# Repricing the matrix engine in a planned instruction order, and turning 64 x 64 blocks by products alone

## Chip, cores and metric

The kernel runs on one core of a Trainium2 chip. The metric is the device time of one execution in microseconds (us). The kernel before took a median of 3212.47 us in three runs (3202.04 to 3217.61).

## What is computed

One inference step of a two-layer decoder trunk, all in fp32, for 256 prompt positions and 8 sample rows that share the weights. They are laid side by side, so every activation has T = 264 columns.

```python
for i in range(DEPTH):
    h = rmsnorm(x, norm_mix[i])
    if i % 2 == 0:
        proj = h @ w_in_a[j]
        o_rwkv, sh, S = rwkv7_mix(proj[..., :RWKV_PROJ], ...)
        o_s5, hr, hi = s5_mix(proj[..., RWKV_PROJ:], ...)
        mix = jnp.concatenate([o_rwkv, o_s5], -1) @ w_out_a[j]
    else:
        mix, S = retention_mix(h @ w_in_c[j], st_ret[j], pos, ret_gn[j], w_out_c[j])
    x = x + mix
    x = x + swiglu(rmsnorm(x, norm_ffn[i]), w_gate[i], w_up[i], w_down[i])
```

Layer 0 mixes with RWKV-7 (16 heads of 64, worked as 8 pairs, in chunks of 64 positions) beside S5 (64 groups of states). Layer 1 mixes with retention.

## The kernel before, in words

**The stream.** All large matrix products are one list of tasks (`run_stream`, L555). A task is one 128-column tile of a weight. Four row blocks of 128 (a grain) arrive by one DMA; ScalarE rounds them to a high part `wh` (L478) and VectorE takes the low part `wl` (L479), and each block is multiplied in three passes, `wh*xh + wh*xl + wl*xh` (L578 to L580). So the stream is matmuls of a 128 x 128 weight with 264 columns, three for each block of 128 rows.

**The side work.** The mixers run beside the stream as Python generators ("sides"): S5, its output, the RWKV fronts, two interleaved RWKV backs, their ends, the sample rows (`rwkv_sample_half`, L1296), and in layer 1 `ret_mix` and `ret_sample`. Their calls are recorded as operations with dependencies (`issue`, L289).

**The order.** Nothing is scheduled on the chip: each engine runs its instructions in the order in which the planner emits them. The planner keeps a clock for each engine (`clk`, keys P, V, S, G and D for TensorE, VectorE, ScalarE, GpSimd and DMA), prices an instruction in `cost` (L213), finds when its operands are ready in `after` (L240), and advances the clock in `emit` (L258). After every second block of 128 rows, `pump` (L519) emits side operations that are ready by the planner's TensorE clock, up to a budget: 1.65 us of that clock in layer 0, 1.3 us in layer 1 (`MOST` times `PART` over `UK`). A stream task that needs a flag of a side has side operations forced out until the flag is there (`need`, L550).

**Prices of TensorE before** (L216 to L227): a stream matmul 0.113 us, a transposition 0.11 us or 0.04 us for 64 columns, a plain fp32 product of a 64-column weight with 64 columns 0.08 us. The price is doubled where the planner takes the clock for low (L273). A change of the tile size within the array has no price, and products on different quarters of the array are priced one after the other. VectorE, ScalarE, GpSimd and DMA have prices of their own (L228 to L238, L265), which the change leaves alone; a DMA is given 1.7 us and 0.03 us plus 1.11e-5 us an element.

**Blocks turned.** RWKV needs 64 x 64 blocks transposed. `turned` (L401) does a block that lands on partitions 0 to 63 by a transposition and one that lands on partitions 64 to 127 by a product with the identity. It is called in `front` (L885: 8 blocks a pair) and through `heads` in `back` for the first level (L946: 8 blocks, L951: 6 blocks, L956: 8 blocks). In all of these calls the two kinds alternate.

**The sample rows.** For each of the 8 pairs, `rwkv_sample_half` multiplies by a matrix of ones (L1349), lets VectorE and GpSimd work on the result (L1350, L1351), spreads a row over 64 partitions by two DMAs into the same tile (L1354), multiplies that tile on VectorE (L1356), adds on GpSimd (L1357), and goes back to TensorE (L1361).

Of the kernel before, what the change touches and what calls it, by code (L numbers as in the profile page):

```python
# [10 lines left out]
F32R = mybir.dt.float32r  # L11
# [9 lines left out]
T = TP + TS  # L21
# [20 lines left out]
FAR = 1 << 20  # L42
# [17 lines left out]
class Task:  # L60
    def __init__(self, w, row0, nk, c0, rhs, done, need=None):
        self.w, self.row0, self.nk, self.c0 = w, row0, nk, c0
        self.rhs, self.done, self.need, self.pre = rhs, done, need, None
# [64 lines left out]
class Builder:  # L128
    def __init__(self, ctx, tc, ins, outs, dumps=None):
        self.ctx, self.tc, self.nc = ctx, tc, tc.nc  # L130
        self.I, self.O, self.C0 = ins, outs, ins["cst"]
        self.dumps = dumps or {}
        self.side, self.rec = [], None
        self.evac = Side(None, -1)
        self.clk = dict.fromkeys("PVSGD", 0.0)
        self.where, self.uses, self.pend = {}, {}, {}
        self.tick, self.cols, self.warm = 0, 0.0, False
        self.flags = Flags(self)
        self.act_set = None
        nc = self.nc  # L140
        self.V, self.G, self.S, self.P = (Eng(self, e, k) for e, k in
                                          ((nc.vector, "V"), (nc.gpsimd, "G"), (nc.scalar, "S"), (nc.tensor, "P")))
        self.Q, self.QG, self.QS = (Eng(self, e, "D") for e in (nc.sync, nc.gpsimd, nc.scalar))
        pool = lambda name, **k: ctx.enter_context(tc.tile_pool(name=name, **k))
        self.pw = pool("pw", bufs=1)
        self.pc = pool("pc", bufs=1)
        self.pb = pool("pb", bufs=1)
        self.ps = pool("ps", bufs=1, space=PSUM)
        ctx.enter_context(tc.manual_schedule())
        self.banks = [self.ps.tile([128, 512], F32, name=f"ps{i}", tag=f"ps{i}") for i in range(8)]  # L150
        self.layer, self.held = 0, {}
        self.turn, self.bank, self.open, self.busy = 0, {}, [], [None] * 4
        for b in self.banks:
            self.cells(b)
# [58 lines left out]
    def cost(self, key, name, a):  # L213

        n = int(np.prod(a[0].shape[1:])) if hasattr(a[0], "shape") else 1
        if key == "P":  # L216
            w = a[2] if name == "transpose" else a[1]
            w = int(np.prod(w.shape[1:]))
            if a[1].dtype == F32R:
                return 0.113 * n / T  # L220
            if name == "transpose":
                return 0.11 if w > 64 else 0.04
            if w <= 32:
                return max(0.034, 0.02 + 0.42e-3 * n)
            if w <= 64:
                return max(0.08, 1.05e-3 * n)
            return max(0.205, 1.68e-3 * n)  # L227
        if key == "V":  # L228
            fast = name in ("tensor_scalar", "tensor_copy", "memset") and not any(str(x.space) == str(PSUM) for x in a if hasattr(x, "space"))
            c = 0.07 + n * (0.52e-3 if fast else 1.04e-3) + (0.006 * n if name == "reciprocal" else 0)  # L230
            if name.startswith(("tensor_scalar", "scalar")) and any(hasattr(x, "shape") and tuple(x.shape[1:]) == (1,) for x in a[2:]):
                c += 0.07
            return c
        if key == "S":
            return 0.094 + n * 0.83e-3
        if key == "D":
            return 0.03 + n * a[0].shape[0] * 1.11e-5
        return 0.035 + n * 0.83e-3 if name == "memset" else 0.15 + n * 2.05e-3  # L238

    def after(self, key, uses):  # L240

        t = 0.0
        for name, (at, bits), w in uses:
            if isinstance(name, int):
                b = self.bank[name].at
                if b is None:
                    name = min((self.banks[i].tensor.name for i in range(4) if not self.busy[i]), key=lambda n: self.uses[n].max())
                else:
                    name = self.banks[b].tensor.name
            u = self.uses[name]  # L250
            for q in (0, 1) if w else (0,):
                for e, k in enumerate("PVSG"):
                    v = u[q, e][at].max()
                    if v:
                        t = max(t, v + (LAG["P" in (k, key)] if k != key else 0.0 if key == "P" or q else 0.125))
        return t

    def emit(self, eng, name, a, k):  # L258

        a = [self.real(x) for x in a]  # L260
        key, uses = eng.key, self.operands(name, a, k)
        c = self.cost(key, name, a)
        t = self.after(key, uses)
        if key == "D":
            t = self.clk["D"] = max(t + 1.7, self.clk["D"]) + c  # L265
        else:
            if key == "P":
                while self.clk["P"] + 0.1 >= (self.tick + 1) * 3.4133:
                    self.warm = self.cols >= 3277
                    self.tick, self.cols = self.tick + 1, 0.0  # L270
                n = int(np.prod(a[0].shape[1:]))
                self.cols += n * (1 if a[1].dtype == F32R else 2 if name == "transpose" else 4) * a[1].shape[0] / 128
                c *= 1 if self.warm else 2  # L273
            elif key == "S":
                self.functions(ACT_SET.get(a[2]))
            t = self.clk[key] = max(self.clk[key], t) + c
        for n, (at, bits), w in uses:
            self.uses[n][0 if w else 1, "PVSG".index(key) if key != "D" else 3][at] = t
        getattr(eng.eng, name)(*a, **k)  # L279
        return t  # L280
# [119 lines left out]

    def turned(self, out, a, one):  # L401

        if out.offset % FAR < out.ap[0][0]:
            self.P.transpose(out, a, one)
        else:
            self.P.matmul(out, a, one, start=True, stop=True)

    def gcopy(self, out, a):
        self.G.tensor_scalar(out, a, 1.0, None, op0=OP.mult)
# [1399 lines left out]
```

## Time and profile before

| what | us |
|---|---|
| median of three runs | 3212.47 |
| lowest, highest run | 3202.04, 3217.61 |
| profiled execution | 3204.68 |
| its span | 3202.9 |
| TensorE busy in the span | 3121.3 |
| VectorE, ScalarE, GpSimd busy | 1972.0, 1498.7, 343.4 |

Every instruction of the planned order has the line of `emit` that issues it (L279), so groups are told apart by tile names and shapes. A form such as `64*64 64x64` is rows * columns of the weight, then partitions x columns of what streams past it. In `ps<-cst,ar_tmp` the operand that streams comes first: a block turned streams the constant identity, `cst`. A plain fp32 product leaves two records, a transposition or a stream matmul one. The timeline gives each piece's start and its duration with the pipeline's drain, so the cost of a piece is read from its start to the start of the next.

### The profile page before, as it was taken

What the parts mean: (1) busy time and instruction counts of PE and PEld (TensorE: products, weight loads), DVE (VectorE), ACT (ScalarE), POOL (GpSimd) and SP (SyncE); (2) the same over time, 40 slices, a digit from 0 to 9 for tenths busy, and PEclk for the clock granted to TensorE, in tenths of its full rate; (3) what the DMA queues carried; (4) which work ended last, traced back from release to release, by engine and by line L of the source; (5) the groups of instructions that cost most, each with busy time, mean ns of one, the idle gap of its engine ahead of it and who ended that gap; (6) DMA issues with size and microseconds to landing.
All of it is one profiled execution on the core that took longest, in us unless ns stands there. A gap on an engine that the chain in (4) does not pass through costs nothing.

```text
span 3202.9 us, 65844 instructions
## 1 busy us (share of the span) xinstructions
PE 3121.3 (97%) x26390; PEld 2967.3 (93%) x26390; DVE 1972.0 (62%) x3702; ACT 1498.7 (47%) x2733; POOL 343.4 (11%) x525
## 2 busy tenths in 40 slices
PE   7999798899999999999999999999999999999998
PEld 7987687799999999999998998988899999999998
DVE  6788666466555555566566666565566565555554
ACT  6543355255444444455344444444455444444454
POOL 5111332100000000001111111011100000000001
PEclk9999899799999999999999999999999999999999
DMA  5323413455655556666666677567666555565654
GB/s 192 120 86 74 61 54 70 84 163 183 179 184 180 182 179 184 181 182 211 216 230 219 230 250 254 174 244 250 217 179 184 181 182 184 178 183 180 184 179 152
DMA packets 161138, 560.54 MB, mean 175 GB/s; under 512 B 21312, under 2 KB 23744, under 8 KB 160576
## 3 DMA queue, kind: packets, MB, share of 16 engines
q1 hardware_dynamic: 140384, 483.29, 50.7%
q0 software_dynamic: 19584, 71.31, 5.9%
q8 instruction: 207, 3.39, 0.4%
q10 hardware_dynamic: 864, 1.74, 0.1%
q14 instruction: 99, 0.81, 0.1%
HBM read 511.45 MB, written 42.69 MB: 173 GB/s over the span
## 4 chain that ended last, share of the span: by engine, by line
PE 92%; DVE 3%; DMA 2%; ACT 1%; POOL 1%; issue 0%; SPq 0%; DVEq 0%; POOLq 0%; ACTq 0%
PE ps L279 92%; DMA ar_tmp<-ar_tmp 2%; DVE ar_tmp L279 1%; POOL ar_tmp L279 1%; DVE wl L279 1%; DVE t L279 1%; ACT ar_tmp L279 0%; ACT wh L279 0%; DVE ar_hidb L279 0%; DVE ar_hidy L279 0%; SPq L279 0%; DVE xl L279 0%; DVE ar_hida L279 0%; POOL ar_hida L279 0%; ACT L285 0%
## 5 line engine op out<-in xcount | busy, mean ns | idle before, releaser
L279 DVE TENSOR_TENSOR wl<-raw,wh 128x512 fp32r<-128x512 f32 x1784 | 1260.6, 710 | 904.1 <-ACT wh L279 892.5
L279 ACT ACTIVATE wh<-raw 128x512 fp32r<-128x512 f32 x1784 | 1098.9, 628 | 936.3 <-PE ps L279 905.5
L279 PE MATMUL ps<-xh,wh 128*128 128x264 f32 x4512 | 1330.0, 295 | 14.7 <-ACT wh L279 12.4
L279 PE MATMUL ps<-xh,wl 128*128 128x264 f32 x4512 | 1289.7, 286 | 10.8 <-DVE wl L279 10.7
L279 PE MATMUL ps<-xl,wh 128*128 128x264 f32 x4512 | 1287.8, 285 | 0.0
L279 PEld LDWEIGHTS ps<-xh,wh 128*128 128x128 f32 x4512 | 858.8, 190 | 63.4 <-issue 28.6
L279 PEld LDWEIGHTS ps<-xh,wl 128*128 128x128 f32 x4512 | 856.4, 190 | 12.6 <-DVE wl L279 12.6
L279 PEld LDWEIGHTS ps<-xl,wh 128*128 128x128 f32 x4512 | 860.0, 191 | 5.7 <-issue 4.8
L279 PE MATMUL ps<-hl,wh 128*128 128x264 f32 x1280 | 364.0, 284 | 0.0
L279 PE MATMUL ps<-hh,wl 128*128 128x264 f32 x1280 | 363.9, 284 | 0.0
L279 PE MATMUL ps<-hh,wh 128*128 128x264 f32 x1280 | 363.8, 284 | 0.0
L279 PE MATMUL ps<-n,wh 128*128 128x264 f32 x1408 | 257.4, 284 | 0.0
L279 PE MATMUL ps<-ar_tmp 64*64 64x64 f32 (+8 forms) x2912 | 215.3, 283 | 39.5 <-DVE ar_tmp L279 24.6
L279 PEld LDWEIGHTS ps<-hh,wh 128*128 128x128 f32 x1280 | 241.4, 189 | 0.0
L279 PEld LDWEIGHTS ps<-hl,wh 128*128 128x128 f32 x1280 | 240.9, 188 | 0.0
L279 PEld LDWEIGHTS ps<-hh,wl 128*128 128x128 f32 x1280 | 240.7, 188 | 0.0
L279 PEld LDWEIGHTS ps<-ar_tmp 64*64 64x64 f32 (+3 forms) x2912 | 149.3, 149 | 82.3 <-DVE ar_tmp L279 28.9
L279 POOL TENSOR_TENSOR sqs<-sq,sqs 128x264 f32<-128x264 f32 x56 | 42.4, 758 | 1663.5 <-ACT sq L279 1663.5
L279 PEld LDWEIGHTS ps<-n,wh 128*128 128x128 f32 x1408 | 217.8, 188 | 0.0
L279 PE MATMUL ps<-n,wl 128*128 128x264 f32 x704 | 199.6, 284 | 0.0
L279 PE MATMUL ps<-omh,wh 128*128 128x264 f32 x512 | 147.1, 287 | 0.0
L279 PE MATMUL ps<-omh,wl 128*128 128x264 f32 x512 | 145.6, 284 | 0.0
(214 smaller groups left out, 2872.1 us busy)
## 6 DMA issues: line engine op xcount, KB each, us to landing
raw<-in_w_in_c_dram SPq DMA_DIRECT2D x192, 512.0 KB, 4.3
raw<-in_ffn_w_gate_dram SPq DMA_DIRECT2D x176, 512.0 KB, 3.6
raw<-in_ffn_w_up_dram SPq DMA_DIRECT2D x176, 512.0 KB, 3.7
raw<-in_ffn_w_down_dram SPq DMA_DIRECT2D x176, 512.0 KB, 3.7
out_dram<-ar_tmp POOLq DMA_DIRECT2D x72, 512.0 KB, 4.3
raw<-in_w_in_a_dram SPq DMA_DIRECT2D x68, 512.0 KB, 3.7
ar_tmp<-in_state_ret_dram POOLq DMA_DIRECT2D x64, 512.0 KB, 6.9
raw<-in_w_out_c_dram SPq DMA_DIRECT2D x64, 512.0 KB, 3.8
```

The source lines that it names most:

```text
L279: getattr(eng.eng, name)(*a, **k)
```

## The change

Three things: new TensorE prices in `cost`; a tile size and a place in the array for each matmul (`tile_of`), by which `emit` adds a price for a change of size, and lets matmuls of one small size on different places overlap in the plan; and `turned` without its transposition. No constant of the planner changes (budgets, look-ahead, priorities), nor any price of another engine.

```diff
@@ def cost(self, key, name, a):
             w = int(np.prod(w.shape[1:]))
+            load = 0.004 + 0.833e-3 * w
             if a[1].dtype == F32R:
-                return 0.113 * n / T
+                return max(load, 0.005 + 0.44e-3 * n)
             if name == "transpose":
-                return 0.11 if w > 64 else 0.04
-            if w <= 32:
-                return max(0.034, 0.02 + 0.42e-3 * n)
-            if w <= 64:
-                return max(0.08, 1.05e-3 * n)
-            return max(0.205, 1.68e-3 * n)
+                return max(load, 0.42e-3 * n)
+            return 2 * max(load, 0.002 + 0.833e-3 * n)
...
+    def tile_of(self, name, a):
+
+        r = lambda n: 32 if n <= 32 else 64 if n <= 64 else 128
+        w = a[1]
+        m = 128 if name == "transpose" or w.dtype == F32R else r(int(np.prod(w.shape[1:])))
+        size = r(int(w.shape[0])), m
+        return size, (w.offset // w.ap[0][0], a[0].offset % FAR // a[0].ap[0][0])
...
@@ def emit(self, eng, name, a, k):
                 c *= 1 if self.warm else 2
+                size, at = self.tile_of(name, a)
+                t0 = max(self.clk["P"], t)
+                if size != self.size:
+                    t0 = max([t0, *self.tiles.values()]) + 0.09 + 0.833e-3 * size[1]
+                    self.size, self.tiles = size, {}
+                t0 = max(t0, self.tiles.get(at, 0.0))
+                t = self.tiles[at] = t0 + c
+                self.clk["P"] = t if size == (128, 128) else t0 + 0.012
             elif key == "S":
                 self.functions(ACT_SET.get(a[2]))
-            t = self.clk[key] = max(self.clk[key], t) + c
+            if key != "P":
+                t = self.clk[key] = max(self.clk[key], t) + c
...
     def turned(self, out, a, one):
 
-        if out.offset % FAR < out.ap[0][0]:
-            self.P.transpose(out, a, one)
-        else:
-            self.P.matmul(out, a, one, start=True, stop=True)
+        self.P.matmul(out, a, one, start=True, stop=True)
```

## Rows read from the trace of the kernel before

**Rows 1.** The page: span, TensorE's busy time, the chain by engine

```profile
span 3202.9 us, 65844 instructions
...
PE 3121.3 (97%) x26390; PEld 2967.3 (93%) x26390; DVE 1972.0 (62%) x3702; ACT 1498.7 (47%) x2733; POOL 343.4 (11%) x525
...
PE 92%; DVE 3%; DMA 2%; ACT 1%; POOL 1%; issue 0%; SPq 0%; DVEq 0%; POOLq 0%; ACTq 0%
```

**Rows 2.** Windows: length, busy us of PE, PEld, DVE, ACT, POOL; PEclk, DMA, GB/s

```profile
0.00:180.00 180.00, 154.45 (x1176) 148.21 (x1177) 135.06 (x303) 107.44 (x212) 55.54 (x101) 0.95 0.47 152
180.00:300.00 120.00, 117.56 (x1340) 100.32 (x1338) 104.25 (x310) 47.45 (x96) 21.09 (x36) 0.97 0.29 77
300.00:420.00 120.00, 98.83 (x1007) 81.95 (x1007) 76.20 (x192) 38.15 (x108) 40.05 (x65) 0.83 0.40 62
420.00:540.00 120.00, 117.56 (x1451) 97.50 (x1449) 81.79 (x214) 73.01 (x153) 41.81 (x68) 0.99 0.21 56
540.00:660.00 120.00, 102.43 (x1125) 85.82 (x1126) 59.39 (x132) 29.25 (x63) 17.01 (x18) 0.80 0.47 88
660.00:740.00 80.00, 79.83 (x659) 79.56 (x658) 59.11 (x106) 46.36 (x94) 10.65 (x15) 1.00 0.58 178
740.00:3202.00 2462.00, 2450.61 (x19641) 2373.95 (x19639) 1456.20 (x2448) 1157.06 (x2010) 157.29 (x224) 1.00 0.63 197
```

**Rows 3.** Groups by form: the matmuls of turned 64 x 64 blocks

```profile
L279 PE MATMUL ps<-cst,ar_tmp 64*64 64x64 f32 x192 | 30.6, 256 | 0.1
...
L279 PE MATMUL ps<-cst,ar_hida 64*64 64x64 f32 x75 | 11.3, 243 | 0.0
...
L279 PE MATMUL ps<-cst,ar_hidb 64*64 64x64 f32 x45 | 7.4, 260 | 1.3 <-DVE ar_tmp L279 1.3
...
L279 PE MATMUL ps<-cst,t 64*64 64x64 f32 x48 | 7.1, 243 | 0.0
```

**Rows 4.** PE timeline: two turned groups, of eight and of six blocks

```profile
184.11 1.36 PE L279 MATMUL ps<-cst,ar_hida 64*64 64x64 f32 x9
185.40 0.39 PE L279 MATMUL ps<-xh,wh 128*128 128x264 f32 x1
...
191.66 0.28 PE L279 MATMUL ps<-xh,wl 128*128 128x264 f32 x1
191.87 1.79 PE L279 MATMUL ps<-cst,ar_hida 64*64 64x64 f32 x12
193.59 0.70 PE L279 MATMUL ps<-ar_hidy,cst 128*128 128x256 f32 x2
```

**Rows 5.** PE timeline: groups of products alone, of eight and six blocks

```profile
242.20 0.68 PE L279 MATMUL ps<-ar_tmp 64*64 64x64 f32 x16 [0.67 <-DVE ar_tmp L279]
242.81 0.39 PE L279 MATMUL ps<-xh,wh 128*128 128x264 f32 x1
243.04 0.28 PE L279 MATMUL ps<-xl,wh 128*128 128x264 f32 x1
...
451.94 0.57 PE L279 MATMUL ps<-ar_hidb,ar_tmp 64*64 64x64 f32 x12 [0.33 <-DVE ar_tmp L279]
452.44 0.39 PE L279 MATMUL ps<-xh,wh 128*128 128x264 f32 x1
```

**Rows 6.** Waits of PE: waited for, us in total, times, longest

```profile
PE ps L279 <- DVE ar_tmp L279: 28.6, 13, 7.3
...
PE ps L279 <- POOL ar_tmp L279: 7.9, 1, 7.9
```

**Rows 7.** Pieces of the chain: the first and last row spread by DMA

```profile
293.02 10.07 DMA ar_tmp<-ar_tmp
...
578.78 10.08 DMA ar_tmp<-ar_tmp
```

**Rows 8.** PE timeline: first and last departure from the stream before 660 us

```profile
29.76 1.25 PE L279 MATMUL ps<-sqs,cst 128*128 128x264 f32 x2
...
658.60 0.60 PE L279 MATMUL ps<-ar_hidx,ar_hida 128*128 128x264 f32 x2
```

More of the change, by code (lines that the diff above doesn't have):

```diff
@@ L137, in __init__ @@
         self.tick, self.cols, self.warm = 0, 0.0, False
+        self.size, self.tiles = None, {}
         self.flags = Flags(self)
```

## The prediction, made before the changed kernel was run

> **What bounds the kernel now.** I read the page first: TensorE is busy for 3121 of 3203 us, and the chain that ends last runs over it for 92% [rows 1]. Then the windows, since such a share mixes stages with different limits [rows 2]. From 740 us on (both feed-forward blocks and layer 1) TensorE has 2451 busy us in 2462, one record every 0.125 us: there only fewer or cheaper matmuls help, and the change touches no block of that stretch except through the order. Up to 660 us, in layer 0, TensorE is still the engine with least room: 98% busy from 180 to 300 us and from 420 to 540 us. Two stretches are looser, 300 to 420 us (99 of 120 us busy) and 540 to 660 us (102 of 120), and in these two the granted clock is 0.83 and 0.80, a mixture of the full 2.4 GHz and the half, 1.2 GHz; elsewhere it is 0.95 or more. VectorE comes close in one stretch alone, 104 of 120 us from 180 to 300 us.
>
> Third, the waits: in the side work TensorE idled 28.6 us for VectorE and 7.9 us for GpSimd [rows 6], 36.5 us together. The chain shows what stands behind most of it: a row spread over the partitions by DMA takes 10.07 us at the first and 10.08 us at the last of the seven pieces of this kind in it, from 293 to 589 us [rows 7]. VectorE runs in order, so while its next instruction waits for that landing, everything behind it waits too, and TensorE with it.
>
> **Turned blocks: the sure part.** Eight pairs turn 8 blocks in the front and 8, 6 and 8 in the back: 24 groups of eight and 8 groups of six, 240 blocks. Half are transpositions (one record), half products (two), so 360 records are due, and the four groups have 192 + 75 + 45 + 48 = 360 [rows 3]. The change removes 120 transpositions and adds 120 products, 120 records more on balance.
>
> What a group costs is read from its start to the next piece's. A mixed group of eight takes 193.59 - 191.87 = 1.72 us for 12 records; a group of eight products takes 242.81 - 242.20 = 0.61 us for 16 [rows 4, 5]. So more records take a third of the time: in the mixed group each record stands apart by 0.14 us, in the uniform one by 0.04. A mixed group of six takes 1.29 us, six products 0.50 us. The gain is 24 x 1.11 + 8 x 0.79 = 33 us, all of it in layer 0. I take it whole, because TensorE has no room there, and the next engine would bind only from 180 to 300 us: some 11 of the 33 us lie there, and 104 us of VectorE still fit in the 109 that remain. Its lower bound is 33 less those 11, if VectorE's queue ends up as the limit of that stretch.
>
> **Repricing, stream and layer 1.** A stream matmul goes from 0.113 to 0.121 us in the plan, next to 0.125 in the rows [rows 2]. The instructions stay; only their places can move. TensorE is full there and VectorE has 1456 of 2462 us, so I take nothing, with bounds of 5 us either way. What covers a later VectorE result is the stream itself; without it each miss costs the shortfall.
>
> **Repricing, layer 0: departures from the stream.** The plan now charges for a change of tile size, and a group of eight products rises from 8 x 0.08 = 0.64 us to some 0.60 plus a change on each side. But TensorE's planned clock moves only 0.012 us at each small product within such a group, so while `pump` is at a group, fewer other operations become ready. A visit then ends sooner, and two backs that now share a departure may take one each. There are 158 departures before 660 us [rows 8]. One more costs the way in, the drain and the slow first step: 0.61 - 16 x 0.03 = 0.13 us after the group, 0.23 - 0.12 = 0.11 us at the first stream matmul [rows 5], and 0.21 - 0.12 = 0.09 us before the group [rows 4], 0.33 us in all. Twenty more would cost 6.6 us. I take +6. Bounds: -10 us (30 fewer) and +30 us (90 more).
>
> **Repricing, layer 0: the spread rows.** The planner gives such a DMA 1.7 us and 0.03 + 512 x 64 x 1.11e-5 = 0.39 us for each of the two, some 2.5 us, where 10.1 us is measured [rows 7], so it is 7.6 us short, 8 times: 61 us. TensorE idles only 36.5 us of that [rows 6]. The other half is hidden by accident: TensorE was priced too low, so the work planned beside the landing really lasts longer than planned. True prices remove that cushion, while VectorE, ScalarE, GpSimd and the DMAs stay underpriced. In the worst case all 61 us show, +24 us; if the landings fall beside other work, the term is -10 us. I take two fifths of the worst case, +10 us, because the work beside a landing is partly stream, and the stream's price rises only 7%.
>
> **Sum.** -33 + 0 + 6 + 10 = -17 us. The profiled execution took 3204.68 us (span 3202.9), so its like would take 3188 us. That execution stands 8 us under the median of 3212.47; between the two ways of counting (3188 and 3195) I say **3190 us**. A measurement of this kernel can tell about 0.5%, 16 us, from no change.
>
> **Rivals.** *The order hardly moves, or improves.* The places of side operations hang on readiness more than on TensorE's price; if both order terms are nil, 33 us are gained: 3172 us against the profiled run, 3180 against the median. If fewer idle stretches keep the clock at its full level, more comes: 0.17 and 0.20 of two 120 us windows were lost to the lower level [rows 2], and half of those 44 us back gives some 3150 us. For it: most departures are set by dependencies. Against it: the landings stay underpriced. The Trainium skill (TensorE: Matmul & The Clock Gate, Part 4: PE-mode transpose) says that transpositions don't count as work for the clock the way matmuls do, which would favour products here. No row tells, since the turned groups are short and stand among other work.
>
> *The order gives everything back: no change.* Both order terms at about two thirds of their upper bounds (20 + 16 us) eat the 33 us: 3208 to 3215 us. For it: the constants of `pump` stand as they stood with the old prices, and the old underpricing was alike on all engines, so the order was consistent; now TensorE alone is true. Against it: TensorE's record waits are few, 13 and 1 in these rows [rows 6], so most side operations have room to be later.
>
> *Slower: the departures multiply.* The mechanism is the 0.012 us step: `pump` returns to the stream after nearly each group. The stream offers 432 places in layer 0 (34 tiles of 16 blocks and 40 of 8, a place every two blocks), of which 158 are used. At 0.33 us, 100 more eat the 33 us; from 150 more on the kernel is slower by over 0.5%; with 200 more it is at about 3212 + 33 = 3245 us. For it: two backs, the S5 output and the sample rows now share visits. Against it: each operation still waits for VectorE or ScalarE as long as before.
>
> *Products cost more and don't overlap.* If 16 records stood 0.14 us apart as the 12 do, a group would take 2.29 us: +0.57 x 24 + 0.43 x 8 = +17 us, 3229 us. The uniform groups speak clearly against it [rows 5]. The Trainium skill (the same page, Terms) puts the transposition mode at four times the speed for fp32, by which each replaced block would cost more and not less. By that alone, with 0.076 us a product in a uniform group (0.61 / 8), the change would add 120 x 0.75 x 0.076 = 7 us in place of -33, some 3218 us. The rows differ with it as used here: the mixed group is the slower one.
>
> **Chances.** Forecast (part given back): 0.36. Order unmoved or better: 0.16. All given back, within 16 us: 0.36. Slower by departures: 0.09. Products dearer: 0.03. So faster by over 0.5% 0.52, within 0.36, slower 0.12. The range leaves out a tenth at each end: from 3160 us (33 us gained and some of the clock) to 3222 us (both order terms near their upper bounds). The forecast's own range is 3175 to 3196 us.
>
> **What would show it.** Right: groups of turned blocks with 480 records instead of 360, eight blocks in 0.6 us and six in 0.5; the stretch from the first stream matmul to the feed-forward block shorter by 15 to 25 us; the stretch after it within 5 us of now; idle time behind VectorE and GpSimd in the side work of 40 to 55 us in place of 36.5; 160 to 200 departures. Wrong in the first step: turned groups still over 1 us. Wrong in the second: departures above 250, or fewer than 150. Wrong in the third: the idle time behind the landings at 36 us or less, or above 61 us. If layer 1 or the feed-forward blocks move by more than 10 us, the plan reaches further than I say.

## The result and the profile after

The changed kernel takes a median of 3256.99 us (3254.71 to 3261.85, four runs) beside 3211.47 us of the kernel before (3202.04 to 3217.61, four runs): 1.0146 times as long, with a 95% interval of 1.0119 to 1.0174. That is 46 us slower, where 3190 us and a gain of some 20 were forecast. It lies outside the range of 3160 to 3222 us. In the changed kernel every planned instruction has line L294 where it had L279.

The page of the changed kernel, against [rows 1]:

```profile
span 3254.6 us, 66122 instructions
...
PE 3109.2 (96%) x26510; PEld 2960.7 (91%) x26510; DVE 1980.7 (61%) x3707; ACT 1496.5 (46%) x2728; POOL 345.6 (11%) x525
...
PE 82%; DVE 7%; issue 4%; DMA 4%; POOL 2%; ACT 1%; SPq 0%; DVEq 0%; POOLq 0%; ACTq 0%
```

TensorE has 120 records more, as forecast, and is busy for 12 us less, yet the span grew by 52 us. Its share of the chain that ends last fell from 92% to 82%: what was added is time in which TensorE waits.

The windows of the changed kernel, cut as in [rows 2] (columns as there):

```profile
0.00:180.00 180.00, 152.20 (x1158) 144.97 (x1158) 132.56 (x299) 107.80 (x212) 54.23 (x100) 0.96 0.47 149
180.00:300.00 120.00, 104.42 (x1274) 90.33 (x1274) 108.01 (x332) 45.82 (x109) 26.29 (x50) 0.89 0.19 55
300.00:420.00 120.00, 82.62 (x878) 69.70 (x879) 62.87 (x152) 31.70 (x84) 34.63 (x53) 0.79 0.41 57
420.00:540.00 120.00, 113.37 (x1564) 96.92 (x1561) 73.19 (x179) 52.55 (x107) 27.03 (x49) 0.97 0.22 69
540.00:660.00 120.00, 89.48 (x1048) 75.96 (x1047) 64.13 (x150) 42.31 (x90) 26.34 (x29) 0.83 0.43 74
660.00:740.00 80.00, 73.11 (x653) 69.91 (x652) 48.36 (x100) 34.81 (x67) 6.06 (x10) 0.94 0.54 147
740.00:3254.00 2514.00, 2494.01 (x19949) 2412.92 (x19947) 1491.59 (x2498) 1181.48 (x2062) 171.03 (x235) 1.00 0.63 195
```

From 180 to 300 us TensorE is busy for 104 us in place of 118, from 300 to 420 us for 83 in place of 99, from 540 to 660 us for 89 in place of 102. VectorE is busy from 180 to 300 us for 108 us in place of 104, so there it is now the fuller engine.

The stream is the same list of matmuls in every kernel here (2592 in layer 0, 6336 in each feed-forward block, 6144 in layer 1). A stage is therefore counted from the start of its first stream matmul to that of the next stage's. Layer 0 went from 722.9 to 760.8 us (+37.9), layer 1 from 920.6 to 934.4 (+13.8); the feed-forward blocks took 770 and 768 us (the last to the end of its stream), the same before and after. Layer 0, split by the distance from the start of one TensorE record to the next in the trace:

| layer 0, us | before | after | difference |
|---|---|---|---|
| stretches over 0.8 us without a new record, less 0.2 each | 65.6 | 116.8 | +51.2 |
| turned blocks | 51.9 | 18.6 | -33.3 |
| last stream record before a departure | 31.2 | 40.1 | +8.9 |
| other stream records | 334.4 | 339.6 | +5.2 |
| other side records | 239.9 | 245.8 | +5.9 |

The products gave what was forecast, and half as much again as that was lost in waiting. Who waited, in the list of waits of the changed kernel (us in total, times, longest):

```profile
DVE ar_tmp L294 <- DMA ar_tmp<-ar_tmp: 73.4, 8, 11.2
...
PE ps L294 <- DVE ar_tmp L294: 70.7, 36, 9.6
...
PE ps L294 <- ACT ar_tmp L294: 11.8, 3, 11.1
...
PE ps L294 <- POOL ar_tmp L294: 0.4, 1, 0.4
```

The same list of the kernel before has, beside [rows 6], this row:

```profile
DVE ar_tmp L279 <- DMA ar_tmp<-ar_tmp: 50.0, 8, 9.1
```

VectorE stands behind the eight spread rows for 73.4 us in place of 50.0, and TensorE behind VectorE for 70.7 in place of 28.6. Both kinds of TensorE's waits behind VectorE grew: by the traces of layer 0, those of more than 3 us from 22.8 us in all (4) to 43.9 (6), the shorter ones from 6.0 (10) to 23.9 (23). One of the eight in the changed kernel, first on VectorE's timeline, then on TensorE's (start us, us, what, and in brackets the idle time before it and what ended it):

```profile
603.10 0.42 DVE L294 TENSOR_TENSOR ar_tmp<-ar_tmp,ps 128x256 f32<-128x256 f32 x1 [0.51 <-PE ps L294]
614.65 0.69 DVE L294 TENSOR_TENSOR ar_tmp<-ar_tmp 128x512 f32<-128x512 f32 x1 [11.13 <-DMA ar_tmp<-ar_tmp]
615.26 0.69 DVE L294 TENSOR_TENSOR wl<-raw,wh 128x512 fp32r<-128x512 f32 x1
615.87 0.41 DVE L294 TENSOR_TENSOR ar_tmp<-ar_tmp,ps 128x256 f32<-128x256 f32 x1
```

```profile
606.22 0.68 PE L294 MATMUL ps<-ar_tmp 64*64 64x64 f32 x16
616.33 1.12 PE L294 MATMUL ps<-ar_tmp 64*64 64x64 f32 x16 [9.43 <-DVE ar_tmp L294]
```

VectorE's next instruction in the list is the multiplication of the spread row (L1356 of the kernel before). It waits 11.13 us for the DMA. Behind it stands, at 615.87 us, an operation for quite another side (by its shape a subtraction of an RWKV back), and TensorE's next group needs that one. So TensorE stops for 9.43 us although its own operands have nothing to do with the DMA.

### The profile page after: what moved, and what is told of

The parts are those of the page before. It is cut to its first block, busy times and chain, and to the rows that moved or that the text cites. A ratio compares the mean times of both kernels' runs of the same rounds, so it can differ in the third digit from the quotient of the medians.

```text
span 3254.6 us, 66122 instructions
## 1 busy us (share of the span) xinstructions
PE 3109.2 (96%) x26510; PEld 2960.7 (91%) x26510; DVE 1980.7 (61%) x3707; ACT 1496.5 (46%) x2728; POOL 345.6 (11%) x525
## 4 chain that ended last, share of the span: by engine, by line
PE 82%; DVE 7%; issue 4%; DMA 4%; POOL 2%; ACT 1%; SPq 0%; DVEq 0%; POOLq 0%; ACTq 0%
PE ps L294 82%; DVE ar_tmp L294 3%; DMA ar_tmp<-ar_tmp 2%; DVE t L294 1%; DVE wl L294 1%; POOL ar_tmp L294 1%; DMA out_dram<-ar_tmp 1%; ACT ar_tmp L294 1%; ACT wh L294 0%; DMA ar_tmp<-in_state_ret_dram 0%; DVE ar_hida L294 0%; POOL sq L294 0%; POOL t L294 0%; SPq L294 0%; DVE ar_hidy L294 0%
## 5 line engine op out<-in xcount | busy, mean ns | idle before, releaser
L294 DVE TENSOR_TENSOR wl<-raw,wh 128x512 fp32r<-128x512 f32 x1784 | 1252.0, 708 | 914.2 <-ACT wh L294 895.2
L294 ACT ACTIVATE wh<-raw 128x512 fp32r<-128x512 f32 x1784 | 1098.0, 627 | 937.0 <-PE ps L294 853.0
L294 PE MATMUL ps<-xh,wh 128*128 128x264 f32 x4512 | 1336.7, 296 | 17.4 <-ACT wh L294 10.7
L294 PE MATMUL ps<-xh,wl 128*128 128x264 f32 x4512 | 1290.9, 286 | 6.0 <-DVE wl L294 6.0
L294 PE MATMUL ps<-xl,wh 128*128 128x264 f32 x4512 | 1288.6, 286 | 1.3 <-DVE xl L294 1.3
L294 PEld LDWEIGHTS ps<-xh,wh 128*128 128x128 f32 x4512 | 859.5, 190 | 73.0 <-issue 40.6
L294 PEld LDWEIGHTS ps<-xl,wh 128*128 128x128 f32 x4512 | 861.5, 191 | 7.4 <-issue 4.8
L294 PEld LDWEIGHTS ps<-xh,wl 128*128 128x128 f32 x4512 | 858.0, 190 | 8.0 <-DVE wl L294 8.0
L294 PE MATMUL ps<-hh,wl 128*128 128x264 f32 x1280 | 363.6, 284 | 0.0
L294 PE MATMUL ps<-hl,wh 128*128 128x264 f32 x1280 | 363.6, 284 | 0.0
L294 PE MATMUL ps<-hh,wh 128*128 128x264 f32 x1280 | 363.5, 284 | 0.0
L294 PE MATMUL ps<-ar_tmp 64*64 64x64 f32 (+7 forms) x2912 | 221.5, 286 | 64.1 <-DVE ar_tmp L294 50.0
L294 PE MATMUL ps<-n,wh 128*128 128x264 f32 x1408 | 257.4, 283 | 0.0
L294 PEld LDWEIGHTS ps<-ar_tmp 64*64 64x64 f32 (+3 forms) x2912 | 152.3, 151 | 104.4 <-issue 45.2
L294 PEld LDWEIGHTS ps<-hh,wh 128*128 128x128 f32 x1280 | 241.2, 188 | 0.0
L294 PEld LDWEIGHTS ps<-hl,wh 128*128 128x128 f32 x1280 | 240.7, 188 | 0.0
L294 PEld LDWEIGHTS ps<-hh,wl 128*128 128x128 f32 x1280 | 240.5, 188 | 0.0
L294 POOL TENSOR_TENSOR sqs<-sq,sqs 128x264 f32<-128x264 f32 x56 | 42.5, 760 | 1686.0 <-ACT sq L294 1686.0
L294 PEld LDWEIGHTS ps<-n,wh 128*128 128x128 f32 x1408 | 217.6, 188 | 0.0
L294 PE MATMUL ps<-n,wl 128*128 128x264 f32 x704 | 199.4, 283 | 0.0
L294 PE MATMUL ps<-omh,wh 128*128 128x264 f32 x512 | 145.9, 285 | 0.0
L294 PE MATMUL ps<-omh,wl 128*128 128x264 f32 x512 | 145.4, 284 | 0.0
```

## The experiments

Each kernel was timed against the kernel before on the same chip. Three edits recur. The landing (planner only; nothing changes on the chip but the order; the planner has one clock for all DMAs, so those issued later are planned later too):

```diff
-            t = self.clk["D"] = max(t + 1.7, self.clk["D"]) + c
+            t = self.clk["D"] = max(t + (9.8 if tuple(a[0].shape) == (64, 512) else 1.7), self.clk["D"]) + c
```

The overlap, in `after`:

```diff
                 for e, k in enumerate("PVSG"):
+                    if k == key == "P":
+                        continue
                     v = u[q, e][at].max()
```

The third is the change's own edit of `turned`. What all of them gave, with stages counted as above in one profiled execution of each, and VectorE's wait for the spread rows from each list of waits (none: no such row):

| kernel | median us | ratio to before (95%) | layer 0 | layer 1 | departures in layer 0 | VectorE behind the rows |
|---|---|---|---|---|---|---|
| before | 3211.47 | | 722.9 | 920.6 | 158 | 50.0 |
| changed | 3256.99 | 1.0146 (1.0119 to 1.0174) | 760.8 | 934.4 | 187 | 73.4 |
| products, old prices | 3177.08 | 0.987 (0.9856 to 0.9885) | 694.2 | 920.6 | 158 | 47.7 |
| new prices, old turning | 3284.59 | 1.0203 (1.0188 to 1.0218) | 795.9 | 931.3 | 221 | 76.1 |
| changed + landing | 3198.17 | 0.9933 (0.9916 to 0.9949) | 701.2 | 937.2 | 187 | 17.2 |
| changed, prices x 0.8 | 3229.33 | 1.0031 (1.0017 to 1.0044) | 732.3 | 936.6 | 138 | 57.9 |
| changed + overlap | 3242.52 | 1.0087 (1.0065 to 1.0108) | 750.4 | 928.4 | 153 | 63.2 |
| changed + both | 3134.47 | 0.9751 (0.973 to 0.9772) | 645.2 | 928.4 | 156 | 1.3 |
| products + landing, old prices | 3122.07 | 0.9714 (0.9689 to 0.9739) | 640.0 | 921.1 | 159 | none |
| both, old stream price | 3135.56 | 0.9752 (0.9727 to 0.9776) | 649.3 | 924.6 | 158 | 2.4 |
| both, no doubling | 3152.94 | 0.981 (0.978 to 0.9841) | 655.3 | 928.4 | 159 | 2.5 |

The kernel before varied between 3202 and 3221 us over all these rounds, with medians of 3211 to 3220, and its profiled execution took 3204.68. A stage's difference from its 722.9 us can be off by some 15 us for that reason (an estimate from these medians).

**The two parts apart.** First the kernel before with the new `turned` alone:

> The kernel before with all blocks turned by products, planned at the old prices. If the products are worth what the uniform groups showed and the loss comes from the prices, about 33 us are gained: 3170 to 3190 us, turned groups of eight at 0.6 us. If products in turned groups are themselves the loss (they don't overlap, or they bring the clock down), 3220 us or more.

3177.08 us, as the first bound says: 43 us under the 3219.75 of the kernel before in these rounds, and 28.7 us less in layer 0 by the two profiles; layer 1 and the departures (920.6 us, 158) are those of before. Then the changed kernel with the old `turned`:

> The changed kernel with the old way of turning blocks (transposition and product in turn), new prices kept. If the two parts add up, the products' 33 us are lost on top: about 3290 us, turned groups of eight at 1.7 us. If the new order is only bad because of the products, about 3210 us.

3284.59 us. Within that spread the parts add up: the products are worth 35 us of layer 0 at the new prices (795.9 to 760.8; 28 by the medians) and 29 at the old ones (43 by the medians). The prices cost 67 us of layer 0 with the products (694.2 to 760.8) and 73 without. The sign of the result is the prices' alone.

**The landing.** The changed kernel, with the DMAs that spread a row planned at what they take:

> The changed kernel, with the two DMAs that spread a sample row planned at some 10.2 us in place of 2.1. If the loss is the landings that lost their cushion, the idle time behind them (about 60 us in the changed kernel) goes to under 25 us: 3215 us or less. If the loss is many short waits on VectorE and more departures, at most 15 us come back: 3242 us or more.

3198.17 us, 59 less than the changed kernel; layer 0 is 60 us shorter, and layer 1 3 us longer. Its list of waits:

```profile
DVE ar_tmp L294 <- DMA ar_tmp<-ar_tmp: 17.2, 6, 8.0
...
PE ps L294 <- DVE ar_tmp L294: 33.1, 34, 4.6
```

VectorE's time behind the landings falls from 73.4 to 17.2 us, TensorE's behind VectorE from 70.7 to 33.1. The result meets the bound of the theory of the landings: nothing on the chip is faster, VectorE's instruction that waits has only moved behind others that are ready. That the landings cost what the new prices lost doesn't follow from it, since the same edit is worth as much at the old prices (below). And it doesn't remove the short waits: in layer 0, those of up to 3 us come to 25 us, after 24 before the edit.

**A cushion for all.** If true prices are the trouble, prices that are all too low should cure it:

> The changed kernel with all TensorE prices of the plan, changes of tile size too, at 0.8 of the new ones. If the loss is that TensorE alone is priced true beside engines that are priced too low, the cushion is back and with the products 3170 to 3200 us come out. If the loss is the form of the new clock (tile sizes, 0.012 us steps, more departures), it stays above 3240 us.

3229.33 us, between the two theories. Departures fall below those of before (138), VectorE's wait for the landings to 57.9 us, and a 28 us gain comes back. A general cushion hides the landings in part, and it is much the poorer tool: the one price that is wrong gives twice as much.

**The planned overlap that isn't.** Working back from layer 1, where nothing is spread by DMA and yet 13.8 us were lost, I found a second fault in the new prices. `tile_of` gives each small matmul its place in the array, so that matmuls on different places may overlap in the plan. But `emit` first takes from `after` the time at which the operands are ready, and there a PSUM bank is one cell, and a matmul is held until the planned end of the one before it in the same bank. Groups of small matmuls write to one bank. Eight products of layer 1 with 32 columns, 512 long, are planned at 8 x 2 x 0.4285 = 6.9 us; in the timeline of the changed kernel the next piece starts after 1.85:

```profile
1613.47 1.92 PE L294 MATMUL ps<-ar_tmp 128*32 128x512 f32 x16
1615.32 0.39 PE L294 MATMUL ps<-xh,wh 128*128 128x264 f32 x1
```

And a group of eight products in layer 0 is planned at 8 x 0.115 = 0.92 us and the changes of size, where 0.62 us are measured (165.27 to 165.89, below). So small groups were not priced true but too high; the old prices of the same groups, 8 x 0.235 = 1.88 and 8 x 0.08 = 0.64 us, were nearer. Where the plan lets VectorE or ScalarE finish beside such a group, TensorE is in fact there sooner, and has to wait. Lifting the rule alone:

> The changed kernel, except that the planner no longer holds a matmul back until the one before it in the same PSUM bank has ended in the plan. In the changed kernel that rule undoes the planned overlap: sixteen small matmuls of layer 1 that take 1.9 us are planned at 6.9. If this overpricing is what layer 1 lost, its 14 us come back and layer 0 loses fewer short waits: 3215 to 3243 us. If overpricing doesn't matter, within 6 us of 3257.

3242.52 us: 14 us back, 10 in layer 0 (departures from 187 to 153) and 6 in layer 1. That is inside the first bound, but less than half of what layer 1 had lost came back, where all of it was expected. The landings stay:

```profile
PE ps L296 <- DVE ar_tmp L296: 75.7, 34, 8.5
...
DVE ar_tmp L296 <- DMA ar_tmp<-ar_tmp: 63.2, 8, 9.8
```

So with the overlap in place, prices that are nearer to the truth still lose 56 us of layer 0 to the old ones (750.4 against 694.2). Both repairs:

> Both repairs, the overlap and the landing at 10.2 us. If the two make up the whole loss of the new prices, it meets the products alone at the old prices (3177 us) or beats it: 3155 to 3182 us. If departures or the rest of the clock cost something of their own, it stays at 3185 us or more.

3134.47 us, better than either bound. Its list of waits:

```profile
PE ps L296 <- DVE ar_tmp L296: 19.0, 24, 1.8
...
DVE ar_tmp L296 <- DMA ar_tmp<-ar_tmp: 1.3, 2, 1.1
```

The two help each other: alone they give 59 and 14 us, together 122. With the landing planned but small groups too dear, the short waits remained (33.1 us behind VectorE in all); with both, 19.0 us.

**The landing with the old prices.**

> Products alone at the old TensorE prices, with the landing planned at 10.2 us. If the old prices hid only part of the landings by accident, as the idle time behind them says (some 40 us), 25 to 40 us are gained on 3177: 3137 to 3152 us. If the cushion hid them well enough, within 10 us of 3177.

3122.07 us, the best kernel of the study and 2.9% under the one before: 55 us less than the products alone, where 25 to 40 were expected. Its list of waits has no row for VectorE behind the spread rows, and for TensorE

```profile
PE ps L279 <- DVE ar_tmp L279: 11.4, 18, 1.3
```

Three of its windows in layer 0, which ends at 649 us:

```profile
180.00:300.00 120.00, 112.22 (x1509) 98.44 (x1508) 112.81 (x339) 46.61 (x94) 24.43 (x42) 1.00 0.32 87
300.00:420.00 120.00, 113.17 (x1500) 97.20 (x1500) 93.72 (x245) 60.50 (x166) 54.11 (x92) 0.99 0.37 70
420.00:540.00 120.00, 112.61 (x1534) 95.45 (x1533) 86.84 (x211) 68.62 (x131) 32.21 (x41) 0.96 0.37 89
```

From 300 to 420 us TensorE is busy for 113 us at a granted clock of 0.99, in place of 83 us at 0.79 in the changed kernel.

Together with the landing planned in the changed kernel, this run tells how much the landing explains. Planning it is worth 55 us at the old prices and 59 at the new, so the landing alone is not what the new prices lost: with it planned, they still cost 61 us of layer 0 (640.0 to 701.2), nearly as much as without (67). Only then lifting the banks' hold takes off 56 of them (701.2 to 645.2), where it takes off 10 without the landing. Either fault alone is enough for most of the loss, which goes only when both are repaired.

12 us remain between this kernel and the one with all new prices and both repairs, 5 in layer 0 and 7 in layer 1. Two runs go into them. The stream's price:

> The kernel with both repairs (overlap and landing), and the stream's matmuls priced at 0.113 us again in place of 0.121. If the stream's price is what layer 1 still loses (928 us in place of 921), layer 1 comes back to within 2 us of 921 and the whole to 3122 to 3130 us. If the new prices of the small matmuls do it, layer 1 stays at 927 us or more.

Neither bound was met. Layer 1 came to 924.6 us, half of the way, and layer 0 grew by 4, so the whole stayed. The stream's price is part of what layer 1 lost, not all of it. And the doubling of prices where the planner takes the clock for low:

> The kernel with both repairs, and TensorE's planned prices never doubled for a low clock. The true prices fill a planned window with less work, so the planner takes the clock for low more often. If that doubling costs, layer 0 gets shorter by 5 us or more (3128 us or less); if not, within 5 us of 3134.

3152.94 us: without the doubling layer 0 is 10 us longer in the profiled execution, and the median 18 us above that of both repairs. The doubling helps, against what was suspected.

## Why the prediction was wrong, point by point

Layer 0 lost 66.6 us to the prices, with the products in both kernels (694.2 to 760.8), where the two order terms had 6 + 10. Of the signs that were named, two of the wrong ones came true: the idle time behind VectorE and GpSimd is 71.1 us, above 61, and layer 1 moved by more than 10 us. The 480 records and the number of departures (187) came as forecast.

**Turned blocks: right.** Forecast were 480 records, eight blocks in 0.6 us and six in 0.5. The timeline of the changed kernel, against [rows 4, 5]:

```profile
165.27 0.68 PE L294 MATMUL ps<-cst,t 64*64 64x64 f32 x16 [0.40 <-DVE t L294]
165.89 0.70 PE L294 MATMUL ps<-ar_hidy,cst 128*128 128x256 f32 x2
...
558.56 0.56 PE L294 MATMUL ps<-cst,ar_hida 64*64 64x64 f32 x12
559.05 0.48 PE L294 MATMUL ps<-ar_tmp,cst 128*128 128x256 f32 x1
```

The groups by form of the changed kernel, against [rows 3], have 256 + 100 + 60 + 64 = 480 records:

```profile
L294 PE MATMUL ps<-cst,ar_tmp 64*64 64x64 f32 x256 | 11.3, 226 | 2.0 <-DVE ar_tmp L294 2.0
...
L294 PE MATMUL ps<-cst,ar_hida 64*64 64x64 f32 x100 | 4.9, 240 | 2.3 <-DVE ar_tmp L294 2.0 <-DVE ar_hida L294 0.2
...
L294 PE MATMUL ps<-cst,ar_hidb 64*64 64x64 f32 x60 | 2.8, 226 | 0.3 <-DVE ar_tmp L294 0.3
...
L294 PE MATMUL ps<-cst,t 64*64 64x64 f32 x64 | 2.7, 224 | 1.5 <-DVE t L294 1.4 <-DVE ar_tmp L294 0.2
```

33.3 us less of turned blocks in the trace, 33 forecast, and 29 and 35 us of layer 0 when only this edit is made or undone. By the rule of the Trainium skill (TensorE: Matmul & The Clock Gate, Terms) that the transposition mode is four times as fast for fp32, the products would have cost time; the two pairs of runs that differ only in how blocks are turned disagree with it, for 64 x 64 blocks among products of the same size.

**The spread rows: the mechanism right, the term mis-sized, and this is the first step that failed.** I took +10 us, between -10 and +24, for TensorE's idle time. In the rows that it was read from, that went from 36.5 to 71.1 us, over the worst case of 61. The term is told best where the small products overlap in the plan as I had read them. There, planning the landing takes 105 us off layer 0 (750.4 to 645.2), and at the old prices 54 (694.2 to 640.0). So half was hidden at the old prices, as I said, but half of 105 us and not of 61: new prices bring out 51 us in place of 10. Two things were left out. The worst case counted only what eight landings are short of, and TensorE's long waits stay within it; the short ones grew by 18 us beside them, and they are not the landings', since they remain when the landings are planned. And the stops cost more than the idle time itself: the granted clock is 0.79 and 0.83 in two windows of the changed kernel, and 0.93 and 0.96 in the same windows of the one with the landing planned:

```profile
300.00:420.00 120.00, 105.62 (x1257) 89.22 (x1257) 82.31 (x203) 46.66 (x123) 48.82 (x75) 0.93 0.43 73
...
540.00:660.00 120.00, 110.50 (x1331) 98.57 (x1330) 76.85 (x166) 45.24 (x89) 21.64 (x23) 0.96 0.60 123
```

The idle of 50 us that VectorE had behind the landings before was on show in the list of waits, and I read only TensorE's rows [rows 6]. Which of TensorE's old prices hid the other half was not tested.

**The hold of the banks: at nothing in the sum, and the second step that failed.** I read a group of eight as some 0.60 us plus changes, where the planner has 0.92 and more: I followed `emit`'s new lines and not `after`, which they start from. With the landing planned, the hold costs 56 us of layer 0 (645.2 to 701.2), by the traces 33 of them in stretches over 0.8 us without a new record, and without it 10 (750.4 to 760.8). In the changed kernel the two faults overlap, so its 67 us can't be divided between them.

**Departures: forecast 6 us for 20 more, measured 29 more, and 8.9 us in the last records before one; the reason given was wrong.** I put them down to the step of 0.012 us. With the overlap really planned, that step works as written, and the departures go down to 153. What raised them was the hold of each bank. Each cost roughly what was forecast: 34 fewer took 8.8 us off all stream records of layer 0 (379.7 to 370.9), 0.26 us each; the drain after a group isn't in that, and the clock has a share in it.

**Layer 1 at nothing, within 5 us: wrong by 13.8 us.** The waits of that stage, where the kernel before has none above 0.1 us:

```profile
PE ps L294 <- POOL t L294: 5.0, 2, 2.6
PE ps L294 <- DVE ar_tmp L294: 3.0, 8, 0.4
```

The stream named as cover was too short before one product of each of the eight heads, that of the rotated q and k. The chain of the changed kernel at one head is below (start us, us, what): GpSimd for 1.85 us, VectorE for 0.72 and 0.72, and TensorE released by them at 1663.33 us. The overlap accounts for 6 us (with it the two waits for GpSimd are gone) and the stream's price for some 4; the rest was not traced.

```profile
1659.94 1.85 POOL ar_tmp L294
...
1661.82 0.72 DVE ar_tmp L294
...
1662.56 0.72 DVE ar_tmp L294
...
1663.33 0.70 PE ps L294 x2
```

**The rivals.** "The order hardly moves" is what the products alone at the old prices show: 3177 us, between its 3172 and 3180; the new prices moved the order. The rival on the slower side named departures; 29 more are far from the 150 that it needed. "The order gives everything back" named landings and departures, 16 and 20 us, and lacked the hold. Its argument, that the old underpricing was consistent and now TensorE alone is true, is borne out for the landing: unpriced, truer prices lose 56 us of layer 0 to the old ones even with the overlap repaired. The range was also narrower than the chances beside it: 0.12 for slower by over 0.5%, above some 3228 us, doesn't go with a tenth above 3222.

**What stays open.** Why the both-repaired kernel is 12 us behind the old prices, 5 of it in layer 0, isn't settled: the stream's price is a part of it in layer 1, and the doubling is not the cause. Each kernel's order is also one draw: of two edits meant for other things, one moved layer 0 by 4 us and one by 10, so differences of that size prove little. Nor was it tried to make the landing itself shorter.

## What to carry to other kernels

In an order that is fixed by a planner, prices matter against each other. Making one engine's prices true can lose what a balance of errors had hidden; look first for the operation whose measured time is furthest from its price (here 10.6 against 2.5 us), and correct that one. Two wrong prices can each be enough for the same loss: a repair that gives 14 us alone gave 64 beside the other, so try repairs together, and try each on the old kernel too before calling it the cause. When a cost model is refined, follow a value through every function that bounds it: an overlap allowed in one place was taken back in another. And where an in-order engine waits long for a DMA, read that engine's own row in the list of waits, not only the row of the engine that is the bound.

## What was not expected of the hardware

A transposition of a 64 x 64 block between products of that size costs far more than a product: 1.72 us for eight blocks that are half transpositions, 0.62 for eight products, though the latter have 16 records for 12. The turn from one kind to the other is the likelier cost, not the transposition: four transpositions of 128 x 128 in a row take 0.35 us in the changed kernel, 0.09 each, beside 0.14 for each record of the mixed group. No run has a row of 64 x 64 transpositions alone, so this is not shown.

```profile
1665.48 0.60 PE L294 MATMUL ps<-cst,ar_tmp 128*128 128x128 f32 x4
1665.83 0.37 PE L294 MATMUL ps<-xh,wh 128*128 128x264 f32 x1
```

And a row spread over 64 partitions within the chip's memory, by two DMAs of 128 KB into one tile, takes 9.98 to 10.59 us at seven of its eight places in the chain of the changed kernel. In that kernel's list of DMAs, from issue to landing, the median is 8.6 us for these and 3.7 to 4.2 for weights of 512 KB from HBM.
